# Turning the recurrence's queries and keys on VectorE and through DRAM instead of on TensorE

## The chip, the cores and the metric

One core of a Trainium2 chip runs the whole program: TensorE (PE; its weight loads are PEld), VectorE (DVE), ScalarE (ACT), GpSimd (POOL) and SyncE (SP), each with its own instruction stream, and DMA queues beside them. The metric is the device time of one execution in microseconds; lower is better. The kernel before takes 2662.75 us (median of 3 runs, 2661.4 to 2662.98).

## The reference, cut to what matters

Two transformer blocks over 256 tokens of width 2048, all float32. The first block projects the normalized input by `w_in` into nine parts; the change concerns the two that feed a gated linear recurrence with 8 heads of 128 channels:

```python
log_f = jnp.log(lb + (1.0 - lb) * jax.nn.sigmoid(z))     # z = h @ w_in, the hf columns
k  = (1.0 - lb) * jax.nn.sigmoid(-z)
qf = jax.nn.silu(q) * (HGRN_DK ** -0.5)                  # q = h @ w_in, the hq columns
...
o_inter = einsum('bhtk,bhkv->bhtv', q_c * exp(b_c), state)      # b_c: running sum of log_f in a chunk
scores  = einsum('bhtk,bhsk,bhtsk->bhts', q_c, k_c, decay)
```

Everything else (window attention, branch products, two feed-forward parts, a top-k mixer and a forgetting mixer) is unchanged.

## The kernel before

The 256 tokens are two tiles of 128. Each projection is cut into chunks of 512 output columns, and each chunk into pieces of 256 input rows. SP loads a piece into a staging half page (`stg`; four halves as a rule). ScalarE casts it to a rounded high part (L283, `ring`), VectorE subtracts to get the low part (L289, which also frees the staging half), and TensorE runs three products per 128 input rows and tile, always in the order A (high by high), B (high by low weight), C (low by high), 512 columns each (L335). A piece so serves 6 products of tile 0 and then 6 of tile 1. Product B cannot start before the piece's low part is there.

The order on every engine is fixed when the program is built. The planner walks the products in order; it emits the cast of a piece when its products are at most 12 units of modelled time away and the subtraction at 11 (`AHEAD_HI`, `AHEAD_LO`). Small work (evacuations, softmax, the recurrence) is written as generators that are pumped once per tick of 1.4 modelled us; `yield n` puts their next part n ticks later. What a generator emits lands between the casts, subtractions and products of that moment, and each engine then runs its list strictly in order.

The first block's order of chunks is hq (first four heads' queries), hf (their gates and keys), hi, hg, then keys and values of the attention, its queries and gates; later the second group of four heads: hq, hf, hi, hg. For a group:

- `head_hq`: after a tile's hq chunk, ScalarE applies Silu (L700) into `q`; four ticks later TensorE turns the four heads by four 128x128 transposes into one PSUM bank (`heads_T`, L350), and ScalarE copies the bank, scaled, into `G["qk"]` (L706).
- `head_hf`: waits for the bounds `lb` and `1-lb`, which POOL loads from `d_lb` (L724); then sigmoids (L730, L731), products with the bounds on VectorE (L734, L735) and POOL (L736), Ln and the rounded high part on ScalarE (L742, L743), the low part on VectorE (L744), and seven ticks later two banks of transposes for the keys, copied by ScalarE (L751).
- `hgrn`: two generators per group; POOL multiplies q by k (L804), TensorE forms running sums (L813, L814), ScalarE exponentiates (L817), POOL and VectorE multiply (L820, L821), TensorE forms the scores (L827).

`prep_lb` computes the bounds once; they are turned on TensorE, copied by VectorE (L494) and written to `d_lb` by POOL (L496). POOL then loads the table of running-sum patterns (L1691, `in_c_L`) and the masks (L1693, `in_c_pick`); ScalarE casts the first (L1695) and POOL the second (L1696). `prep_rope` (L452 to L470) puts a run of some twenty small instructions on VectorE at the same time.

The feed-forward parts already use another way to turn a 128x512 tile: VectorE transposes 32x32 blocks, POOL writes the tile to DRAM, and POOL reads it back with the blocks moved:

```python
nc.vector.transpose(ts, src)                                            # L366, flip_out
self.mq.dma_start(d, ts)                                                # L370
self.mq.dma_start(tr.rearrange("p (i x) -> p i x", i=4),
                  d.rearrange("(i r) (j x) -> (r j) i x", i=4, j=4))    # L376, flip_in
```

`FLIP_OUT` is 5 ticks and `FLIP_IN` 10. A read waits on POOL's queue until its write has landed.

## Time and profile before

| What | Value |
|---|---|
| Time, median of 3 runs | 2662.75 us |
| The profiled execution's own time | 2657.43 us |
| Its span | 2655.6 us |
| PE busy | 2623.4 us (99%) |
| DVE / ACT / POOL busy | 1613.8 (61%) / 1339.5 (50%) / 361.8 us (14%) |
| L335 products | 10824, 2508.7 us busy |
| L350 transposes | 252, 40.8 us busy |
| L366 / L370 / L376 (the existing turns) | 66 each |
| Mean granted TensorE clock | 0.998 |

TensorE is busy nearly all of the span, so a change matters by what it takes from TensorE's list and by what it makes TensorE wait for. Busy shares of the other engines say little: what counts is when a piece's cast and subtraction are done relative to the product that needs them. Times of rows below are microseconds from the start of the span.

### The profile page before, as it was taken

To read this page: it belongs to the slowest core of one execution; us is meant where nothing else is said; L and a number is where in the kernel's file an instruction comes from. 1 tells how busy PE (TensorE), PEld (TensorE's weight loads), DVE (VectorE), ACT (ScalarE), POOL (GpSimd) and SP (SyncE) were. 2 spreads that over 40 slices of the span, in tenths; PEclk is the share of its full clock that TensorE was granted. 3 is DMA by queue.
4 is the path that set the end of the run, shared out by engine and by line. 5 is a ranking of instruction groups with operands and counts; after the bars stand their busy time and mean duration, and the time that the engine had idled before them with its cause. 6 is when DMAs were issued, how large, how long until landed. Compare 5 with 4: busy or idle time off the path is not lost.

```text
span 2655.6 us, 32471 instructions
## 1 busy us (share of the span) xinstructions
PE 2623.4 (99%) x11929; PEld 2168.9 (82%) x11929; DVE 1613.8 (61%) x2145; ACT 1339.5 (50%) x2004; POOL 361.8 (14%) x420
## 2 busy tenths in 40 slices
PE   8999999999999999999999999999999999999998
PEld 7887788888888888888887788788888888888887
DVE  6765676465555454545457564855557757575757
ACT  6545654454553443443435574554556636464644
POOL 1341031020100000000001110100013212121211
PEclk9999999999999999999999999999999999999999
DMA  7545445666676565656566666456556766575754
GB/s 256 165 129 171 161 147 185 221 230 243 219 243 219 212 210 206 217 201 223 209 209 220 235 213 184 137 175 214 191 198 235 250 221 237 209 242 207 246 202 146
DMA packets 154431, 547.02 MB, mean 206 GB/s; under 512 B 19512, under 2 KB 22096, under 8 KB 153248
## 3 DMA queue, kind: packets, MB, share of 16 engines
q1 hardware_dynamic: 133504, 476.83, 51.9%
q0 software_dynamic: 19472, 67.54, 7.8%
q8 instruction: 93, 1.52, 0.2%
q10 hardware_dynamic: 1296, 0.59, 0.1%
q14 instruction: 66, 0.54, 0.1%
HBM read 514.46 MB, written 30.43 MB: 205 GB/s over the span
## 4 chain that ended last, share of the span: by engine, by line
PE 95%; ACT 1%; DVE 1%; POOL 1%; issue 1%; DMA 0%; SPq 0%; ACTq 0%; POOLq 0%; DVEq 0%
PE mm L335 89%; PE sd L350 1%; PE sd L827 1%; DVE ring L289 1%; ACT ring L283 0%; PE sd L1272 0%; PE sd L1349 0%; POOL s L820 0%; ACT s L394 0%; PE sd L670 0%; PE sd L1381 0%; PE sd L627 0%; PE sd L1244 0%; DMA s<-in_x_dram 0%; PE sd L813 0%
## 5 line engine op out<-in xcount | busy, mean ns | idle before, releaser
L335 PE MATMUL mm<-ring,s 128*128 128x512 f32 (+1 forms) x10824 | 2508.7, 391 | 8.0 <-ACT ring L283 6.3
L335 PEld LDWEIGHTS mm<-ring,s 128*128 128x128 f32 x10824 | 2023.4, 188 | 430.8 <-ACT ring L283 7.6
L289 DVE TENSOR_TENSOR ring<-stg,ring 128x1024 fp32r<-128x1024 f32 (+1 forms) x904 | 1088.9, 1252 | 406.2 <-ACT ring L283 399.4
L283 ACT CAST ring<-stg 128x1024 fp32r<-128x1024 f32 (+1 forms) x904 | 904.5, 1049 | 159.3 <-PE mm L335 93.8
L370 POOL DMA_DIRECT2D flip<-s x66 | 37.0, 562 | 973.0 <-DVE s L366 967.4
L1231 ACT ACTIVATE s<-mm,ss 128x512 f32<-128x512 f32 x60 | 41.5, 691 | 237.6 <-PE mm L335 224.9
L1068 DVE TENSOR_TENSOR s<-mm,s 128x512 f32<-128x512 f32 x72 | 48.7, 687 | 86.5 <-PE mm L335 86.3
L1020 ACT ACTIVATE s<-mm,ss 128x512 f32<-128x512 f32 x22 | 15.2, 690 | 139.1 <-PE mm L335 139.1
L1033 DVE SCALAR_TENSOR_TENSOR s<-mm,ss,s 128x512 f32<-128x512 f32 x22 | 16.1, 730 | 108.3 <-PE mm L335 108.3
L345 POOL TENSOR_TENSOR small<-small,mhalf 128x1 f32<-128x1 f32 (+1 forms) x27 | 17.5, 649 | 361.3 <-DVE small L344 328.7
L820 POOL TENSOR_TENSOR s<-s,s 128x512 f32<-128x512 f32 x32 | 53.3, 1672 | 93.8 <-ACT s L817 89.1
L356 ACT CAST s<-sd 64x256 fp32r<-64x256 f32 (+2 forms) x34 | 16.0, 470 | 88.6 <-PE sd L350 49.7
L376 POOL DMA_DIRECT2D s<-flip x66 | 50.5, 767 | 67.8 <-DMA flip<-s 39.8
L394 ACT ACTIVATE s<-sd,cols 128x128 fp32r<-128x128 f32 x160 | 45.8, 388 | 22.0 <-PE sd L350 19.1
L357 DVE TENSOR_TENSOR s<-s,s 128x512 fp32r<-128x512 f32 x22 | 15.2, 690 | 65.3 <-ACT s L356 65.3
L1584 POOL TENSOR_TENSOR s<-s,s 128x512 f32<-128x512 f32 x22 | 41.2, 1874 | 82.9 <-DVE s L1567 82.8
L350 PE MATMUL sd<-ident,s 128*128 128x128 f32 x252 | 40.8, 285 | 9.9 <-DMA ident<-in_c_ident_dram 4.0
L350 PEld LDWEIGHTS sd<-ident,s 128*128 128x128 f32 x252 | 32.4, 147 | 20.7 <-DMA ident<-in_c_ident_dram 4.0
L1565 ACT ACTIVATE s<-s,cols 128x256 f32<-128x256 f32 x88 | 48.2, 594 | 1.5
L357 DVE TENSOR_TENSOR s<-sd,s 64x256 fp32r<-64x256 f32 (+2 forms) x34 | 18.7, 549 | 47.4 <-ACT s L356 47.3
L1587 ACT CAST s<-s 128x512 fp32r<-128x512 f32 x22 | 13.6, 620 | 66.7 <-POOL s L1584 66.7
L366 DVE STREAM_TRANSPOSE s<-s 128x512 f32<-128x512 f32 x66 | 46.2, 706 | 1.6
(293 smaller groups left out, 1247.4 us busy)
## 6 DMA issues: line engine op xcount, KB each, us to landing
stg<-in_w_in_dram SPq DMA_DIRECT2D x232, 512.0 KB, 4.4
stg<-in_w_gu_dram SPq DMA_DIRECT2D x176, 512.0 KB, 5.5
stg<-in_w_dn_dram SPq DMA_DIRECT2D x176, 512.0 KB, 5.4
stg<-in_w_up_dram SPq DMA_DIRECT2D x176, 512.0 KB, 5.3
flip<-s POOLq DMA_DIRECT2D x66, 256.0 KB, 2.6
s<-flip POOLq DMA_DIRECT2D x66, 256.0 KB, 5.7
stg<-in_w_out_dram SPq DMA_DIRECT2D x32, 512.0 KB, 5.7
stg<-in_w_pg_dram SPq DMA_DIRECT2D x32, 512.0 KB, 5.5
```

The source lines that it names most:

```text
L283: nc.scalar.copy(w[:, 0, :, 0 : cc.n], stg[n_hi][0][:, :, 0 : cc.n])
L289: nc.vector.tensor_tensor(wl[:, :, 0 : cc.n], unstage(n_lo)[:, :, 0 : cc.n], wh[:, :, 0 : cc.n].bitcast(F32), op=ALU.subtract)
L335: nc.tensor.matmul(c.ps[t][:, 0 : c.n], xl if p == "C" else xh, wl if p == "B" else wh, start=n == 0, stop=n == 6 * c.nhp - 1)
L350: self.nc.tensor.transpose(bank[:, a * P : (a + 1) * P], s, self.ident)
L366: nc.vector.transpose(ts, src)
L376: self.mq.dma_start(tr.rearrange("p (i x) -> p i x", i=4), d.rearrange("(i r) (j x) -> (r j) i x", i=4, j=4))
L394: nc.scalar.activation(hi[:, a], b3[:, a], AF.Copy, scale=g[a])
L820: nc.gpsimd.tensor_tensor(k3, d3, kt[:, None, :].to_broadcast([P, 4, P]), op=ALU.mult)
L1068: nc.vector.tensor_tensor(y, ps[t], y, op=ALU.add)
L1231: nc.scalar.activation(r, ps[t], AF.Copy, scale=self.rs[t])
L1565: nc.scalar.activation(v, u, AF.Identity, scale=w[2], bias=self.cols[:, C_CB + k : C_CB + k + 1])
L1584: nc.gpsimd.tensor_tensor(o, o, g, op=ALU.mult)
```

## The change

The transposes of `head_hq` and `head_hf` leave TensorE: each of the eight 128x512 tiles (two of queries and two of keys in each of two groups) goes through `flip_out` and `flip_in`, and ScalarE copies from the tile that came back. Since 32x32 blocks come back in another order, the hq and hf columns of `w_in` are permuted on the host, `prep_lb` writes the bounds in that order by four DMAs instead of one, and the high and low parts of log f are written back in the old order through strided views. `hgrn` waits, when the program is built, until the copies have been emitted. The matrix products are unchanged in number.

```diff
 prep_lb
-        self.mq.dma_start(self.d_lb.rearrange("a (h k) -> (a h) k", h=8), q)
+        for n in range(4):
+            self.mq.dma_start(bass.AP(tensor=self.d_lb.tensor, offset=self.d_lb.offset + 512 * n, ap=[[32, 4], [P, 4], [1, 32]]),
+                              q[4 * n : 4 * n + 4].rearrange("p (j r) -> p j r", j=4))
...
 head_hq
-            yield 4
-            bank = yield from self.get("sd")
-            self.heads_T(q, bank)
-            self.drop(q)
-            nc.scalar.activation(G["qk"][:, 0:1024].rearrange("p (h n) -> p h n", h=4)[:, :, t * P : (t + 1) * P],
-                                 bank.rearrange("p (h n) -> p h n", h=4), AF.Copy, scale=P ** -0.5)
-            self.put("sd")
+            ts, d = yield from self.flip_out(q)
+            yield FLIP_OUT
+            tr = yield from self.flip_in(d)
+            self.drop(ts)
+            yield FLIP_IN
+            nc.scalar.activation(self.heads(G["qk"][:, 0:1024], t), tr.rearrange("p (i a q) -> p a i q", i=4, a=4), AF.Copy,
+                                 scale=P ** -0.5)
...
 head_hf
-                nc.scalar.copy(hi[:, u], fs[2 * u])
-                nc.vector.tensor_tensor(lo[:, u], fs[2 * u], hi[:, u].bitcast(F32), op=ALU.subtract)
-            yield 7
+                f4 = fs[2 * u].rearrange("p (j h r) -> p j h r", j=4, h=4)
+                hi4, lo4 = (z[:, u].rearrange("p (h r j) -> p j h r", h=4, j=4) for z in (hi, lo))
+                nc.scalar.copy(hi4, f4)
+                nc.vector.tensor_tensor(lo4, f4, hi4.bitcast(F32), op=ALU.subtract)
...
-                self.heads_T(fs[2 * u + 1], bank)
...
+                outs.append((yield from self.flip_out(fs[2 * u + 1])))
+            yield FLIP_OUT
...
+                trs.append((yield from self.flip_in(d)))
+            yield FLIP_IN
+            for u in range(2):
+                nc.scalar.copy(self.heads(G["qk"][:, 1024:2048], u), trs[u].rearrange("p (i a q) -> p a i q", i=4, a=4))
...
 hgrn
+        for f in (f"q{g}0", f"q{g}1", f"k{g}"):
+            yield from self.wait(f)
...
 _layout
+    for z in (1536, 2560):
+        w_in[:, z : z + 1024] = w_in[:, z : z + 1024].reshape(2048, 2, 4, 4, 32).swapaxes(2, 3).reshape(2048, 1024)
```

On TensorE the only difference is that eight banks of transposes are gone; on SP nothing moves. Three places on the other engines matter for the prediction.

VectorE, first group, around the gates. Before, from the second tile's products with the bounds (L734, L735) on; `ring_575` is the low part of the fourth piece of the chunk hi:

```order
L734 TENSOR_TENSOR s_55_586<-s_55_586,s_54_583 128x512
L735 SCALAR_TENSOR_TENSOR s_55_586<-s_55_586,s_54_583 128x512
L744 TENSOR_TENSOR s_56_599<-s_54_583,s_56_599 128x512
L744 TENSOR_TENSOR s_56_599<-s_55_586,s_56_599 128x512
L289 TENSOR_TENSOR ring_575<-stg_126,ring_575 128x1024
```

The same place of the changed kernel (L740, L741 are the products, L752 the low parts, `ring_577` is the same piece):

```order
L740 TENSOR_TENSOR s_56_588<-s_56_588,s_55_585 128x512
L741 SCALAR_TENSOR_TENSOR s_56_588<-s_56_588,s_55_585 128x512
L752 TENSOR_TENSOR s_57_601<-s_55_585,s_57_601 128x4x128
L752 TENSOR_TENSOR s_57_601<-s_56_588,s_57_601 128x4x128
L366 STREAM_TRANSPOSE s_56_588<-s_55_585 128x512
L366 STREAM_TRANSPOSE s_56_588<-s_56_588 128x512
L289 TENSOR_TENSOR ring_577<-stg_126,ring_577 128x1024
```

The two block transposes of the keys stand between the gates and the piece's subtraction.

POOL, first group, before: the bounds written (L496), the two tables loaded, the masks cast, the bounds read back (L724):

```order
L345 TENSOR_TENSOR small<-small,mhalf 128x1
L540 COPY ss_77<-small 128x1
L496 DMA d_lb<-s_31_311 16x128
L1691 DMA s_46_489<-in_c_L_dram 128x1152
L1693 DMA s_47_491<-in_c_pick_dram 128x1024
L1696 CAST pm<-s_47_491 128x1024
L724 DMA s_54_583<-d_lb 128x512 x2
```

And of the changed kernel, from the first tile's write on (L345 and L542 make the second tile's normalization factor):

```order
L370 DMA flip_392<-s_31_311 128x512
L345 TENSOR_TENSOR small<-small,mhalf 128x1
L542 COPY ss_77<-small 128x1
L370 DMA flip_411<-s_40_409 128x512
L497 DMA d_lb<-s_31_311 4x4x32 x4
L376 DMA s_31_311<-flip_392 128x4x128
L376 DMA s_40_409<-flip_411 128x4x128
L1706 DMA s_47_489<-in_c_L_dram 128x1152
L1708 DMA s_48_491<-in_c_pick_dram 128x1024
L1711 CAST pm<-s_48_491 128x1024
L730 DMA s_55_585<-d_lb 128x512 x2
```

The loads of both tables now stand behind five more DMAs, and a write of a flip stands ahead of the second tile's factor.

ScalarE, first group, before: the table cast, four pieces cast, then the gates' sigmoids:

```order
L1695 CAST s_45_488<-s_46_489 128x1152
L283 CAST ring_527<-stg_121 128x1024
L283 CAST ring_543<-stg_121 128x1024
L283 CAST ring_559<-stg_126 128x1024
L283 CAST ring_575<-stg_126 128x1024
L730 ACT_TABLE_LOAD
L730 ACTIVATE s_54_583<-mm_408,ss_77 128x512
```

And of the changed kernel, where L711 are the two copies of the queries:

```order
L1710 CAST s_46_488<-s_47_489 128x1152
L283 CAST ring_527<-stg_121 128x1024
L283 CAST ring_543<-stg_121 128x1024
L283 CAST ring_559<-stg_126 128x1024
L711 ACTIVATE s_37_389<-s_31_311 128x4x128
L711 ACTIVATE s_37_389<-s_40_409 128x4x128
L283 CAST ring_577<-stg_126 128x1024
L736 ACT_TABLE_LOAD
L736 ACTIVATE s_55_585<-mm_415,ss_77 128x512
```

The copies of the queries moved from right after their products to just ahead of the last cast before the sigmoids.

## Rows read from the trace of the kernel before

**Rows 1.** Waits of TensorE over the span: total, times, longest, all us
```profile
PE mm L335 <- ACT ring L283: 6.3, 3, 3.7
PE mm L335 <- DVE ring L289: 1.5, 2, 1.0
```

**Rows 2.** Chain in order of time, first group: start us, us, what
```profile
40.08 0.44 PE sd L350 x4
...
42.35 25.88 PE mm L335 x114
...
70.48 13.64 PE mm L335 x60
...
88.65 0.84 PE sd L827 x8
```

**Rows 3.** Costliest groups of the page, and its DMA issues with landing
```profile
L376 POOL DMA_DIRECT2D s<-flip x66 | 50.5, 767 | 67.8 <-DMA flip<-s 39.8
...
L366 DVE STREAM_TRANSPOSE s<-s 128x512 f32<-128x512 f32 x66 | 46.2, 706 | 1.6
...
flip<-s POOLq DMA_DIRECT2D x66, 256.0 KB, 2.6
s<-flip POOLq DMA_DIRECT2D x66, 256.0 KB, 5.7
```

**Rows 4.** DMA issues by line, the read of the bounds
```profile
s<-d_lb POOLq DMA_DIRECT2D x4, 256.0 KB, 4.2
```

**Rows 5.** Timeline of VectorE, first group: start, us, engine, line, operation, idle before
```profile
40.41 1.23 DVE L289 TENSOR_TENSOR ring<-stg,ring 128x1024 fp32r<-128x1024 f32 x1 [1.46 <-ACT ring L283]
...
63.23 0.69 DVE L734 TENSOR_TENSOR s<-s 128x512 f32<-128x512 f32 x1 [1.92 <-ACT s L730]
...
69.48 0.69 DVE L744 TENSOR_TENSOR s<-s,s 128x512 fp32r<-128x512 f32 x1 [0.75 <-ACT s L743]
70.08 5.17 DVE L289 TENSOR_TENSOR ring<-stg,ring 128x1024 fp32r<-128x1024 f32 x4
```

**Rows 6.** Timeline of ScalarE, first group
```profile
38.75 0.69 ACT L700 ACTIVATE s<-mm,ss 128x512 f32<-128x512 f32 x1
...
53.62 1.16 ACT L1695 CAST s<-s 128x1152 fp32r<-128x1152 f32 x1 [2.92 <-DMA s<-in_c_L_dram]
...
60.14 1.05 ACT L283 CAST ring<-stg 128x1024 fp32r<-128x1024 f32 x1 [0.21 <-DMA stg<-in_w_in_dram]
...
62.50 0.69 ACT L730 ACTIVATE s<-mm,ss 128x512 f32<-128x512 f32 x1
...
72.19 1.07 ACT L751 COPY s<-sd 128x512 f32<-128x512 f32 x2
...
81.43 0.69 ACT L767 ACTIVATE s<-mm,ss 128x512 f32<-128x512 f32 x1
```

**Rows 7.** Timeline of POOL, first group
```profile
39.03 0.56 POOL L345 TENSOR_TENSOR small<-small,mhalf 128x1 f32<-128x1 f32 x1 [5.22 <-DVE small L344]
...
48.09 0.57 POOL L1691 DMA_DIRECT2D s<-in_c_L_dram  x1
48.65 0.54 POOL L1693 DMA_DIRECT2D s<-in_c_pick_dram  x1
55.69 1.04 POOL L1696 CAST pm<-s 128x1024 uint8<-128x1024 f32 x1 [6.50 <-DMA s<-in_c_pick_dram]
...
85.64 1.80 POOL L820 TENSOR_TENSOR s<-s,s 128x512 f32<-128x512 f32 x1 [11.47 <-ACT s L817]
```

**Rows 8.** Timeline of VectorE, second group
```profile
323.05 4.62 DVE L289 TENSOR_TENSOR ring<-stg,ring 128x1024 fp32r<-128x1024 f32 x4
```

**Rows 9.** Timeline of TensorE, second group
```profile
322.99 3.00 PE L335 MATMUL mm<-ring,s 128*128 128x512 f32 x12
```

**Rows 10.** TensorE by stretches: us, busy (instructions), granted clock, DMA share, GB/s
```profile
1441.60:1445.50 3.90, 0.20 (x1) 1.00 0.71 255
1445.50:1448.40 2.90, 2.88 (x7) 0.50 0.41 90
```

More of the change, by code (lines that the diff above doesn't have):

```diff
@@ L686, in grp, with heads @@
         return self.hg[g]
-    def heads_T(self, src, bank):
-        self.transposes(bank, [src[:, a * P : (a + 1) * P] for a in range(4)])
+    @staticmethod
+    def heads(v, t):
+        return v.rearrange("p (h t i q) -> p h t i q", h=4, t=2, i=4)[:, :, t]
     def head_hq(self, c, g):
@@ L742, in done @@
                 nc.scalar.activation(fs[2 * u], fs[2 * u], AF.Ln)
[L743 to L745 removed]
+                f4 = fs[2 * u].rearrange("p (j h r) -> p j h r", j=4, h=4)
+                hi4, lo4 = (z[:, u].rearrange("p (h r j) -> p j h r", h=4, j=4) for z in (hi, lo))
+                nc.scalar.copy(hi4, f4)
+                nc.vector.tensor_tensor(lo4, f4, hi4.bitcast(F32), op=ALU.subtract)
             while "qk" not in G:
                 yield 1
+            outs = []
             for u in range(2):
[L749 to L755 removed]
+                outs.append((yield from self.flip_out(fs[2 * u + 1])))
+                self.drop(fs[2 * u])
+            yield FLIP_OUT
+            trs = []
+            for ts, d in outs:
+                trs.append((yield from self.flip_in(d)))
+                self.drop(ts)
+            yield FLIP_IN
+            for u in range(2):
+                nc.scalar.copy(self.heads(G["qk"][:, 1024:2048], u), trs[u].rearrange("p (i a q) -> p a i q", i=4, a=4))
+            self.drop(*trs)
+            self.flags.add(f"k{g}")
         return done
```

10 lines of the change are left out of this document (3 added, 7 removed).

## The prediction

> **What bounds the kernel now.** I read the page for the engines' shares first, then the waits of TensorE, then the chain in order of time through the first block, then the timelines of the four engines around the places that the change touches, because the share alone would mislead. TensorE is the bound, and over the whole span it waited only 6.3 us for casts and 1.5 us for low parts [rows 1]. So anything taken off TensorE's list is gained in full, and any wait made for it is lost in full. The reader should see in the chain that the first group's part is nothing but products, with banks of transposes between them [rows 2], and in the timelines that VectorE and ScalarE meet their deadlines there with very little to spare.
>
> **What is removed.** Eight banks of four transposes. The chain gives 0.44 us to a bank [rows 2], so 8 x 0.44 = 3.5 us leave TensorE; four banks are the first group's, four the second's, 1.76 us each. The eight copies from PSUM become eight copies from SBUF, which I price alike: 1.07 us for two [rows 6].
>
> Here the Trainium skill speaks against the change. The page VectorE: DVE Perf Modes, section Rules for kernel authors, says to turn 128x128 on TensorE if a PSUM destination will do, and in The three transpose paths it gives 390 ns to one on TensorE in isolation; by that price alone the 32 would free an estimated 12.5 us. In the chain four of them take 0.44 us, so the measured 3.5 us stands in the sum, and by the page's price the total below would come out near zero.
>
> **What is added beside other work.** Eight block transposes on VectorE at 0.71 us [rows 3], eight writes and eight reads on POOL's queue, landing after 2.6 and 5.7 us [rows 3], 4 MB in all. VectorE and POOL have idle time, so these cost nothing as work. The three more writes of the bounds cost an issue each, nearest 0.54 to 0.57 us [rows 7]. Strided writing of log f I price at nothing, since the block copies of the page's turns are strided too; a bound from above is one more pass of 0.69 us per low part [rows 5], which would go into the waits below. What matters is what stands behind the new instructions.
>
> **First group, step 1: the table comes later.** Before, the first tile's Silu ends at 38.75 + 0.69 = 39.44 [rows 6]. Now VectorE turns it to about 40.2. The second tile's factor (0.56 us and a small copy) started at 39.03 [rows 7]; it now stands behind that turn on VectorE and behind the flip's write on POOL and starts near 40.8, so the second Silu runs from 41.65 instead of 40.27, and its turn ends at about 43.05. Behind it on VectorE waits the subtraction that started at 40.41 [rows 5], then the small rope instructions, then the copy that the write of the bounds needs. All of these come 2.6 us later. On POOL the load of the table stood right behind that write, at 48.09 [rows 7]; it comes 2.6 us later, plus three writes (1.7), plus two reads of flips (2 x 0.77 [rows 3]) = 53.9. Its data took 53.62 - 48.09 = 5.5 us before [rows 6, 7]. The two reads, 0.5 MB, go down the same queue just ahead of it, and the masks' load took 7.0 us (48.65 to 55.69) behind the table [rows 7]; I take 6.6 us, between the two, so ScalarE's cast of the table starts at 60.5 instead of 53.62.
>
> Behind this cast on ScalarE stand the pieces of the chunk hi. The table's cast holds ScalarE about 1.06 us and a piece's about 0.98 (one is 1.05, overlapping the next). The second piece is then cast at 62.6 and subtracted by 63.85. Its products started at 42.35 + 90 x 25.88 / 114 = 62.8 [rows 2]; two banks less bring that to 61.9. TensorE waits about 2.0 us, for the cast and then for the low part, where it waited for nothing.
>
> **Step 2: the fourth piece comes later still.** ScalarE casts the third piece (64.5), copies the two query tiles (65.6), casts the fourth (66.5), loads a table (1.28) and starts the sigmoids at 67.8; before it was 62.50 [rows 6], so 5.3 us later. The masks land at about 54.5 + 8 = 62.5; with their cast (1.04) and two issues the bounds arrive about 64.6 + 4.2 = 68.8 [rows 4, 7], which costs a tenth more. From the sigmoids the gates took until 69.48 + 0.69 = 70.17 [rows 5], now 75.6. Behind them stand two block transposes, 1.4 us, and only then the fourth piece's subtraction: from 76.9 to 78.1. Its product B was due at 70.48 + 7 x 0.227 = 72.1 [rows 2], with a margin of 0.7 us over the subtraction that ended about 71.4 (a quarter of the 5.17 us after 70.08) [rows 5]. With four banks gone it is due at 70.3. So TensorE waits 78.1 - 70.3 = 7.8 us by then, the 2.0 us of step 1 among them, the rest in one wait of almost 6 us.
>
> If the table comes no later than before, only the two copies (1.1) and two transposes (1.4) push the subtraction: it ends at 73.8 and the wait is 3.5 us. If the table takes as long as the loads and reads at their slowest, 2 to 3 us more, the wait is 10 to 11 us. I keep 3.5 and 11 as ends and take 7.8.
>
> **Step 3: the clock.** After a stretch of 3.9 us in which TensorE did only 0.20 us of work, the granted clock was 0.50, the lower of its two levels, for 2.9 us [rows 10]. At half speed that loses 1.45 us, and a little more until full speed is back; I take 1.7 us once, after the wait of step 2. From below it is nothing, if no stretch is idle long enough; from above twice that.
>
> **Step 4: the keys.** Their turns end at about 77, the writes land by 80, the reads by 86. ScalarE reaches the two key copies only after the hi evacuation, which started at 81.43 [rows 6] and is bound to TensorE: 81.43 - 1.76 + 9.5 = 89.2. So the landing is hidden by 3 us. But the copies, 1.07 us, now stand ahead of the first exponential. POOL's product came 85.64 + 1.80 - 81.43 = 6.0 us after that evacuation [rows 6, 7], and TensorE's use at 88.65 [rows 2] left about a microsecond; I price what is left at 0.2 us.
>
> **Second group.** The same order with no table in the way: one query copy (0.55) and two block transposes (1.4) stand ahead of the first subtraction of the four that started at 323.05 [rows 8]. It then ends near 326.2. Its piece starts with the second six of the twelve products at 322.99 [rows 9], product B at 324.6; without the two banks of keys that is 323.7. TensorE waits 2.5 us. Ends: 1 us, if the softmax beside it leaves slack, and 4 us. The query flips are long back by then.
>
> **Sum.** -3.5 + 7.8 + 1.7 + 0.2 + 2.5 = +8.7 us. The profiled execution took 2657.43 us of its own, 1.8 more than the span and 5.3 less than the median, so 2666.1 for it, and 2671.5 against the median of 2662.75. With the ends of the terms: -3.5 + 3.5 + 0 + 0 + 1 = +1 and -3.5 + 11 + 3.4 + 0.5 + 4 = +15.4; not all go one way, so this case's own range is 2665.5 to 2677.
>
> **The rivals.** First: the table's load is not late. POOL's queue was idle between its DMAs and the loads of weights pause while VectorE is held, so the data may come in the shadow. Then steps 1 and 2 make 3.5 us: -3.5 + 3.5 + 1.7 + 2.5 = +4.2, 2667.0. Against it: the load needs the copy behind the rope, and that is behind both turns.
>
> Second, on the other side: TensorE's relief is all that counts. The place is the fourth piece's subtraction; it decides whether this ends before 70.3. Against the first rival it would have to be 3.5 us earlier still, by the pieces' weights arriving sooner (their casts before the sigmoids waited for DMA, 0.21 us before the last [rows 6]) and by two PSUM copies less ahead of them. Then nothing is lost, the second group's deadline is met too, and the time is 2662.75 - 3.5 = 2659.2. For it speaks that TensorE waited so little in the whole program [rows 1]; against it, that the margin was 0.7 us.
>
> Third: the flips' reads come late behind the weights and ScalarE stands at the key copies. From a landing of 89.2 on, each microsecond is one on TensorE; 3 us of it and a late table make +14, 2676.8.
>
> **How the numbers follow.** About 0.2% (5.3 us) is what a measurement of this kernel can tell from no change. Forecast 0.55, first rival 0.22, second 0.13, third 0.10. The forecast lies past +5.3 us in all but a tenth of its cases, the first rival in a third: slower 0.68. The second rival reaches -5.3 us only if a bank was worth more than 0.44 and the small waits of the recurrence go too: faster 0.05; the same 0.27. The range for 8 in 10 is 2662.5 to 2677.5: it takes in the first rival and leaves most of the second and the worst of the third out.
>
> **What would show it.** In the changed kernel's waits of TensorE: two to three waits near 62 us for cast and low part, one of 4 to 7 us near 72 for L289 in VectorE, then a lower granted clock for some 3 us; one of 1 to 4 us near 324. On ScalarE the table's cast near 60.5 behind its DMA, on VectorE the two transposes right ahead of the late subtraction. No transposes of L350 between 38 and 71. If TensorE waits under 2 us by 75, steps 1 and 2 are wrong and the time is below 2663; if the table is cast by 56, step 1 is.

## The result, and the profile after

The changed kernel takes 2676.05 us (median of 4 runs, 2674.24 to 2677.69), the kernel before, run on the same chip, 2662.07 (4 runs, 2660.82 to 2662.98): 14.0 us slower, ratio 1.0051, 95% interval 1.0039 to 1.0063. The forecast was 2671.5 in a range of 2662.5 to 2677.5. The sign, the places and the order of events came out; the size did not, 14.0 us for 8.7.

One sentence of the section on the change is wrong: the strided views write the parts of log f in the order in which the turned channels come to lie on the partitions, not in the old one. No step of the working rests on it. And a name: TensorE runs 12 products to a piece and 96 to a chunk, and the product that waited for `ring_577` was its 242nd, so the piece that the text ahead calls the fourth of the chunk hi is its fifth. The recorded expectations use the same names, so "fourth" and "fifth" stand below for that piece and the next; the times are those of the piece meant.

TensorE's waits over the whole span, to be read beside [rows 1]; the columns are total, times, longest:

```profile
PE mm L335 <- ACT ring L283: 9.9, 4, 3.7
PE mm L335 <- DVE ring L289: 8.9, 5, 3.5
PE sd L350 <- ACT ring L283: 2.4, 1, 2.4
```

Casts went from 6.3 to 9.9 us, low parts from 1.5 to 8.9: 11.0 more. Where they stand, in the timeline of TensorE (start, us, instructions, the wait before them):

```profile
65.39 0.50 PE L335 MATMUL mm<-ring,s 128*128 128x512 f32 x1 [3.63 <-ACT ring L283]
66.64 11.34 PE L335 MATMUL mm<-ring,s 128*128 128x512 f32 x36 [0.76 <-DVE ring L289]
81.47 13.94 PE L335 MATMUL mm<-ring,s 128*128 128x512 f32 x53 [3.49 <-DVE ring L289]
...
337.75 1.46 PE L335 MATMUL mm<-ring,s 128*128 128x512 f32 x5 [3.20 <-DVE ring L289]
```

Three places: 3.63 + 0.76 us for chunk hi's second piece, 3.49 us for its fourth, 3.20 us in the second group. Before, TensorE waited at none of the three. The other engines at the first two places, ScalarE first, then VectorE, then POOL (to be read beside [rows 5 to 7]):

```profile
63.23 1.15 ACT L1710 CAST s<-s 128x1152 fp32r<-128x1152 f32 x1 [10.52 <-DMA s<-in_c_L_dram]
67.13 1.15 ACT L711 ACTIVATE s<-s 128x512 f32<-128x512 f32 x2
70.53 0.69 ACT L736 ACTIVATE s<-mm,ss 128x512 f32<-128x512 f32 x1
```

```profile
77.98 1.12 DVE L752 TENSOR_TENSOR s<-s,s 128x512 fp32r<-128x512 f32 x1 [0.78 <-ACT s L751]
79.00 1.30 DVE L366 STREAM_TRANSPOSE s<-s 128x512 f32<-128x512 f32 x2
80.23 4.60 DVE L289 TENSOR_TENSOR ring<-stg,ring 128x1024 fp32r<-128x1024 f32 x4
```

```profile
53.79 0.57 POOL L1706 DMA_DIRECT2D s<-in_c_L_dram  x1
64.30 1.04 POOL L1711 CAST pm<-s 128x1024 uint8<-128x1024 f32 x1 [9.40 <-DMA s<-in_c_pick_dram]
```

The table's load is issued at 53.79 (48.09 before), its cast starts at 63.23 (53.62 before) behind a landing of 9.4 us; the sigmoids follow at 70.53 (62.50 before), and the fourth piece's subtraction stands at 80.23 right behind the two block transposes.

TensorE by stretches, with the columns of [rows 10] (us, TensorE's busy time, ..., granted clock, DMA share, GB/s):

```profile
66.00:72.80 6.80, 6.16 (x15) 4.82 (x16) 4.50 (x7) 6.77 (x10) 1.28 (x2) 0.50 0.82 261
83.10:86.40 3.30, 3.30 (x10) 2.53 (x9) 1.83 (x3) 1.04 (x1) 1.33 (x2) 0.50 0.91 323
339.10:342.40 3.30, 3.30 (x7) 1.94 (x7) 2.02 (x3) 1.48 (x4) 1.39 (x2) 0.50 0.93 304
452.00:455.30 3.30, 3.30 (x10) 2.57 (x9) 3.30 (x5) 0.73 (x1) 0.10 (x1) 0.54 0.20 68
```

Behind each of the three places the granted clock was 0.50, the lower level, for 3.3 us, behind the first for twice that. Half of the busy time is lost: 6.16 / 2 = 3.1 us, and twice 1.65. The last row follows a wait that the change didn't make (2.4 us at 448, 2.1 us before); before, the clock stayed at 1.00 there.

So the profiled spans (2655.6 and 2672.5, +16.9) add up: banks -3.5, waits 7.9 + 3.2, half clock 3.1 + 1.65 + 1.65, the fourth stretch 1.65 + 0.3; together +16.0, and 0.9 is spread. The page shows the two sides: L350 with 32 transposes less (252 and 40.8 us before), and L335, whose number is the same and whose 2508.7 us grew by half clock:

```profile
L335 PE MATMUL mm<-ring,s 128*128 128x512 f32 (+1 forms) x10824 | 2515.2, 392 | 18.9 <-ACT ring L283 9.9
L350 PE MATMUL sd<-ident,s 128*128 128x128 f32 x220 | 35.9, 286 | 10.2 <-DMA ident<-in_c_ident_dram 4.2
```

The profiled execution of before was among its fastest (2657.43; single executions in all the comparisons below took 2656.9 to 2667.3), which is why its profile lies 16.9 us from the other one and the medians 14.0. One execution of experiment 12 ran at a granted clock of 0.60 on average and took 4113.56 us; it counts in the median of the table below and not in the ratio.

### The profile page after: what moved, and what is told of

Its sections match the earlier page's. It is cut to its first block, busy times and chain, and to the rows that moved or that the text cites. A ratio compares the mean times of both kernels' runs of the same rounds, so it can differ in the third digit from the quotient of the medians.

```text
span 2672.5 us, 32451 instructions
## 1 busy us (share of the span) xinstructions
PE 2629.1 (98%) x11897; PEld 2169.8 (81%) x11897; DVE 1619.9 (61%) x2153; ACT 1340.9 (50%) x2004; POOL 372.4 (14%) x439
## 4 chain that ended last, share of the span: by engine, by line
PE 91%; ACT 2%; DVE 2%; issue 2%; POOL 1%; DMA 1%; SPq 0%; ACTq 0%; POOLq 0%; DVEq 0%
PE mm L335 86%; ACT ring L283 1%; PE sd L350 1%; PE sd L842 1%; DVE ring L289 1%; POOL s L835 0%; PE sd L1287 0%; PE sd L1364 0%; DMA s<-in_c_L_dram 0%; ACT s L394 0%; PE sd L672 0%; PE sd L1396 0%; PE sd L629 0%; PE sd L1259 0%; DMA s<-in_x_dram 0%
## 5 line engine op out<-in xcount | busy, mean ns | idle before, releaser
L335 PE MATMUL mm<-ring,s 128*128 128x512 f32 (+1 forms) x10824 | 2515.2, 392 | 18.9 <-ACT ring L283 9.9
L335 PEld LDWEIGHTS mm<-ring,s 128*128 128x128 f32 x10824 | 2028.1, 189 | 446.3 <-ACT ring L283 11.6
L370 POOL DMA_DIRECT2D flip<-s x74 | 41.6, 563 | 1020.5 <-DVE s L366 1011.9
L345 POOL TENSOR_TENSOR small<-small,mhalf 128x1 f32<-128x1 f32 (+1 forms) x27 | 17.5, 649 | 356.3 <-DVE small L344 324.2
L376 POOL DMA_DIRECT2D s<-flip x74 | 56.6, 766 | 65.1 <-DMA flip<-s 32.8
L366 DVE STREAM_TRANSPOSE s<-s 128x512 f32<-128x512 f32 x74 | 51.7, 706 | 8.9 <-ACT s L704 7.2
L350 PE MATMUL sd<-ident,s 128*128 128x128 f32 x220 | 35.9, 286 | 10.2 <-DMA ident<-in_c_ident_dram 4.2
L400 DVE SCALAR_TENSOR_TENSOR s<-sd,cols,s 128x128 fp32r<-128x128 f32 x160 | 44.0, 342 | 3.0 <-ACT s L394 3.0
```

Source lines behind the costliest of these rows:

```text
L335: nc.tensor.matmul(c.ps[t][:, 0 : c.n], xl if p == "C" else xh, wl if p == "B" else wh, start=n == 0, stop=n == 6 * c.nhp - 1)
L350: self.nc.tensor.transpose(bank[:, a * P : (a + 1) * P], s, self.ident)
L376: self.mq.dma_start(tr.rearrange("p (i x) -> p i x", i=4), d.rearrange("(i r) (j x) -> (r j) i x", i=4, j=4))
L400: nc.vector.scalar_tensor_tensor(lo[:, a], b3[:, a], g[a], hi[:, a].bitcast(F32), op0=ALU.mult, op1=ALU.subtract)
```

## The experiments

Each was timed against the kernel before on the same chip; its ratio (of the means) and interval are to that. An interval reaches 2 to 4.5 us to either side, so theories that lie closer together are told apart by the traces and not by the time.

| Kernel | Time, us | Before, us | Ratio, interval |
|---|---|---|---|
| changed | 2676.05 | 2662.07 | 1.0051, 1.0039 to 1.0063 |
| 1 tables first | 2673.42 | 2661.31 | 1.0049, 1.0037 to 1.0062 |
| 2 subtraction first | 2678.82 | 2661.31 | 1.0068, 1.0055 to 1.0080 |
| 3 banks left out of before | 2662.63 | 2661.31 | 1.0008, 0.9999 to 1.0016 |
| 4 order mended | 2684.76 | 2661.31 | 1.0100, 1.0084 to 1.0117 |
| 5 reads after tables | 2675.46 | 2660.63 | 1.0055, 1.0042 to 1.0068 |
| 6 queries only | 2671.22 | 2660.63 | 1.0036, 1.0022 to 1.0050 |
| 7 second group only | 2667.43 | 2660.63 | 1.0019, 1.0010 to 1.0028 |
| 8 order mended again | 2678.94 | 2660.63 | 1.0065, 1.0052 to 1.0077 |
| 9 tables in the middle | 2672.16 | 2661.97 | 1.0038, 1.0026 to 1.0051 |
| 10 and gates later | 2668.59 | 2661.97 | 1.0028, 1.0018 to 1.0037 |
| 11 banks left out, gates later | 2661.54 | 2661.97 | 1.0000, 0.9992 to 1.0009 |
| 12 as 10, copies later | 2671.46 | 2661.61 | 1.0033, 1.0020 to 1.0046 |

**1. Tables first.**

```diff
-                yield 4
+                yield 16
                 nc.scalar.copy(self.L[:, 0 : 9 * P], raw[:, 0 : 9 * P])
...
+                self.spawn(L())
                 self.spawn(self.prep_lb())
...
-                yield 6
-                self.spawn(L())
             self.spawn(later())
```

> The changed kernel, with POOL's two loads of the recurrence's tables issued at the start of its list instead of behind the writes of the bounds and the reads of the turned queries; nothing else moves on any engine. Theory 'order' (work comes late because of what stands ahead of it): ScalarE casts the table before 56 us instead of at 63.2, and the first two waits of TensorE near 62 to 67 us (3.6 and 0.8) go with the 6.7 us at half clock that follow. The fourth piece's subtraction still stands behind the copies of the queries and the two block transposes, and ends at 75 to 75.6 against a use that comes at 70.4: one wait of 4.5 to 5.2 us near 71, then about 3.3 us at half clock (1.65 lost). The second group keeps its 3.2 us and its 1.65. Sum -3.5 + 4.9 + 1.65 + 4.85 = +7.9, so about 2670 (2668.5 to 2671.5). Theory 'traffic' (the turns' bytes crowd the memory, so that weights and tables come late wherever they stand): a wait of about 3 us for a cast stays near 62 and the time is within 2 us of 2676.

Measured: 2673.42, above the 2671.5 that "order" allowed and inside no theory's band. TensorE's timeline:

```profile
11.98 1.97 PE L350 MATMUL sd<-ident,s 128*128 128x128 f32 x8 [5.29 <-DMA s<-in_x_dram]
...
80.16 14.84 PE L335 MATMUL mm<-ring,s 128*128 128x512 f32 x53 [6.68 <-DVE ring L289]
```

The first two waits are gone; the table is cast at 55.95. But POOL had nothing ahead of the loads, so they ran at the start beside the input's, and the first products came 3.0 us later (5.29 us of waiting for `in_x` where 2.39 stood). And the fourth piece's wait grew from 3.49 to 6.68: with TensorE no longer held up at the second piece, it reached the fourth sooner than the subtraction did. Removing one wait handed most of it to the next.

**2. Subtraction first.**

```diff
+            yield 2
             outs = []
...
-            yield FLIP_OUT
+            yield FLIP_OUT - 2
```

> The changed kernel, with the keys' two block transposes two ticks later on VectorE and everything behind them at its old place: in both groups one subtraction of a weight piece passes ahead of the two transposes, and nothing else moves on any engine. Theory 'order': the first waits (3.6 and 0.8) and their half clock stay; the wait near 78 shrinks by the 1.3 us of the transposes from 3.5 to 2.2, the one near 335 from 3.2 to 1.9, and the half clock behind each may stay or go: 2673.4 if both stay, 2670.1 if both go. Theory 'bystanders' (the late subtraction waits for its cast or its data, and the transposes fill time that it would have waited anyway): 2676 and the same waits.

Measured: 2678.82, by the medians 17.5 us over before (14.0 for the changed kernel; the intervals overlap), so no gain, which neither theory gave. TensorE's timeline:

```profile
81.87 12.35 PE L335 MATMUL mm<-ring,s 128*128 128x512 f32 x53 [2.67 <-DVE ring L289]
101.12 1.97 PE L843 MATMUL sd<-s,s 128*128 128x64 f32 x8 [2.37 <-POOL s L836]
...
340.62 1.43 PE L335 MATMUL mm<-ring,s 128*128 128x512 f32 x5 [1.78 <-DVE ring L289]
346.04 2.08 PE L672 MATMUL sd<-s,s 128*128 128x512 f32 x2 [3.99 <-ACT s L665]
```

The two waits for subtractions did shrink, to 2.67 and 1.78, so the transposes are no bystanders. But two new ones, 2.37 for POOL's product of keys (L836) and 3.99 for ScalarE's L665, took more than that. ScalarE, ahead of the first of them:

```profile
89.36 1.05 ACT L283 CAST ring<-stg 128x1024 fp32r<-128x1024 f32 x1 [2.97 <-DMA stg<-in_w_in_dram]
...
94.64 1.13 ACT L767 COPY s<-s 128x512 f32<-128x512 f32 x2
```

The copies of the keys (L767) waited for nothing, so this is not the third rival. ScalarE's casts ahead of them waited for weights, and the copies came 1.25 us later than in the changed kernel (93.39); TensorE, this time without half clock behind the subtraction, stood at the scores' running sums 1.2 us sooner (94.06 for 95.25). In the second group the writes of the turned keys came later by the edit, and L665's tile was still being written to DRAM: L666 right behind it waited 0.70 us for such a write, and 4 shows the same wait of L665.

**3. Banks left out of before.**

```diff
-            bank = yield from self.get("sd")
-            self.heads_T(q, bank)
+            bank = q
...
-                bank = yield from self.get("sd")
-                self.heads_T(fs[2 * u + 1], bank)
+                bank = fs[2 * u + 1]
```

> The kernel before, with the eight banks of four transposes on TensorE left out and nothing in their place: ScalarE's copies read the queries and keys as they lie, so the recurrence gets them unturned. All other engines' lists are unchanged. This is what the removal alone is worth. By the chain's 0.44 us to a bank it is 3.5 us, 2658.6; by the group's mean of 0.162 us for each of 32 transposes 5.2 us, 2656.9. By the margin theory (the fourth piece of the chunk hi was 0.7 us early, and TensorE comes there 1.8 us sooner) a wait of about 1.1 us appears near 70 and perhaps another in the second group, so 2659 to 2661.

Measured: 2662.63, no gain at all (0.9999 to 1.0016).

```profile
73.79 13.98 PE L335 MATMUL mm<-ring,s 128*128 128x512 f32 x53 [3.19 <-DVE ring L289]
```

At the fourth piece TensorE now waited 3.19 us for VectorE and lost about 1.7 more at half clock. The margin theory had the place and was short on the size (1.1 us). What made the size is not the deadline alone. Product B was due at 70.6, 1.5 us sooner than before (72.1), against a margin of 0.7; but the subtraction also ended 2.4 us later than before, though nothing had been put ahead of it. VectorE's list ran 1.1 us later in this execution (L494 at 47.95 for 46.85), and the bounds landed late, by 1.3 more:

```profile
65.74 0.69 DVE L732 TENSOR_TENSOR s<-s 128x512 f32<-128x512 f32 x1 [3.21 <-DMA s<-d_lb]
```

So that the removal alone brings nothing here is shown by the time; that the earlier deadline is the reason, only in part. The 3.5 us that the change was to free could not be had from this order even for nothing.

**4. Order mended.** The edit of 1, and

```diff
             yield from self.wait("lb")
+            yield 2
...
-            yield FLIP_IN
+            yield FLIP_IN + 5
             nc.scalar.activation(self.heads(G["qk"][:, 0:1024], t), ...
...
+            yield 2
             outs = []
...
-            yield FLIP_OUT
+            yield FLIP_OUT - 4
```

> The changed kernel with four things moved and nothing added: tables loaded first on POOL, the gates' sigmoids and products two ticks later (so that one more weight piece is cast and subtracted ahead of them), the keys' block transposes two ticks later still (behind one more subtraction), the copies of the queries five ticks later (behind the gates on ScalarE). Theory 'order': the three waits near 62, 78 and 335 us and the half clock behind them go, and at most 0 to 2 us are left near 73; -3.5 + 0 to 2, so 2658.6 to 2660.6, faster than the changed kernel by 15 to 17 us and at or just below the kernel before. Theory 'traffic': the same bytes move at the same places, so waits for casts stay and the time is above 2668.

Measured: 2684.76, the slowest of all; "order" failed as I had applied it.

```profile
98.83 1.97 PE L844 MATMUL sd<-s,s 128*128 128x64 f32 x8 [5.25 <-POOL s L837]
...
345.07 2.08 PE L672 MATMUL sd<-s,s 128*128 128x512 f32 x2 [7.08 <-ACT s L665]
```

ScalarE's list at the two places:

```profile
91.38 0.62 ACT L768 COPY s<-s 128x512 f32<-128x512 f32 x1 [1.07 <-DMA s<-flip]
...
344.43 0.59 ACT L665 COPY s<-sd 128x512 f32<-128x512 f32 x1 [4.12 <-DMA flip<-s]
```

Of the three waits of the changed kernel 0.9 + 1.4 + 0.9 us were left by 80 us and nothing in the second group's subtraction, as forecast. In their place stood 5.25 us for the scores, with ScalarE standing at the key copies for the reads to land (1.07 us, and 0.86 at the second: the third rival's mechanism), and 7.08 us for L665: ScalarE held its whole list for a tile that a turn's write (L370) was still reading, and that write had been moved back by my own two ticks.

**5. Reads after tables.**

```diff
-            yield FLIP_OUT
+            yield FLIP_OUT + 3
             tr = yield from self.flip_in(d)
...
-            yield FLIP_IN
+            yield FLIP_IN - 3
```

> The changed kernel, with POOL's two reads of the turned queries issued behind its loads of the two tables instead of ahead of them; no other engine's list moves. Theory 'order': without 0.5 MB ahead of it in the queue the table needs about 5.5 us again; issued near 52.2 it is cast at 57.7 to 58.5 instead of 63.2, and TensorE's waits near 62 to 67 us with their 6.7 us at half clock go. What is left is what the kernel with early tables showed, a wait of 5 to 6.7 us for the fourth piece's low part, its half clock, and the second group's 3.2 + 1.65, but without that kernel's 2.9 us at the start: 2669.5 to 2671.5. Theory 'traffic' (what counts is how many bytes POOL's queue and the weights ask for in these 10 us, not their order): the table still takes 8 to 9 us, a wait of 1 to 3 us for the cast stays and the time is 2673 to 2676.

Measured: 2675.46, as the changed kernel, in the band of "traffic" but not by its mechanism: the wait for a cast was gone. The table was cast at 60.34, 7.0 us after its issue (between the theories' 5.5 and 8 to 9), the first wait fell to 0.64, and the fourth piece's rose to 9.78. TensorE, and VectorE's first product with the bounds:

```profile
81.99 14.62 PE L335 MATMUL mm<-ring,s 128*128 128x512 f32 x53 [9.78 <-DVE ring L289]
```

```profile
71.93 0.69 DVE L740 TENSOR_TENSOR s<-s 128x512 f32<-128x512 f32 x1 [4.98 <-DMA s<-d_lb]
```

This shows a second late chain beside the table's: the masks land late too, POOL casts them, and only behind that cast does it issue the bounds' read; VectorE stood 4.98 us for the bounds. In the changed kernel ScalarE's lateness covered this.

**6. Queries only.** `head_hf` and `prep_lb` are those of before, and

```diff
-    for z in (1536, 2560):
+    for z in (1536,):
```

The turned queries' channels then lie in another order than the keys', so this kernel's scores are not the reference's.

> Only the queries are turned on VectorE and through DRAM; the keys keep their four banks on TensorE, the bounds their one write and the gates their plain layout. Theory 'order': the table comes 1.7 us sooner than in the changed kernel (three writes less ahead of it), cast near 61.5, so a first wait of about 2.7 us; the fourth piece's subtraction has no block transposes and no strided writes ahead of it, so the second wait is about 2.7 us; 1.65 us of half clock behind one or both; the second group's wait is under 1 us. -1.76 + 5.4 + 1.65 to 3.3 + 0.5 = +5.8 to +7.4, so 2668 to 2669.5. Theory 'keys' (the keys' turn makes the loss, the queries' is free because nobody waits for them before 85 us): -1.76, 2660.3.

Measured: 2671.22 (2665.55 to 2675.7, a wide spread), above the 2668 to 2669.5 of "order", far above the 2660.3 of "keys". So the queries' turn alone, which nobody needs before 85 us, costs 10.6 of the 14.0 us by the medians (5.9 to 13.3 by the interval), by what it pushes back. TensorE waited 1.07 + 0.76 at the second piece, then 3.20 at a bank of keys (L350), for POOL's product with bounds that had come late.

**7. Second group only.** The first group has the lines of before, and the second group's bounds are written once more, turned, after the first group has read its own:

```diff
+            if g == 0:
+                bank = yield from self.get("sd")
+                self.heads_T(q, bank)
...
-    for z in (1536, 2560):
+    for z in (2048, 3072):
```

> Only the second group of four heads is turned on VectorE and through DRAM; the first group keeps its banks, its tables' place, its plain bounds and its plain gates. Theory 'order': no wait near 62 or 72; near 335 the changed kernel's wait of 3.2 us and its 3.3 us at half clock (1.65 lost). -1.76 + 3.2 + 1.65 = +3.1, 2664.4. Theory 'first group alone' (all of the loss comes from the table and its followers, and the second group's wait was a late effect of it): -1.76, 2659.6.

Measured: 2667.43 (1.0010 to 1.0028); "first group alone" falls.

```profile
326.50 1.43 PE L335 MATMUL mm<-ring,s 128*128 128x512 f32 x5 [3.20 <-DVE ring L289]
```

```profile
328.00:331.50 3.50, 3.50 (x7) 2.14 (x8) 1.85 (x2) 0.37 (x1) 1.25 (x2) 0.53 0.90 267
440.00:446.00 6.00, 6.00 (x23) 4.83 (x22) 5.08 (x9) 1.38 (x2) 0.77 (x1) 0.72 0.50 162
```

The wait is 3.20 us, to the hundredth that of the changed kernel, with its half clock. The profiled span is 4.8 us over that of before: the +3.1 forecast and another 1.6 from the half clock at 440 to 446 (a clock of 0.72 on average), the stretch behind the wait that was there before. The medians differ by 6.8, the means by 5.1. The other 2 us go with half clock: the three executions with a granted clock of 0.997 or 0.998 on average took 2662.2 to 2663.1, the eight with 0.994 to 0.996 took 2665.1 to 2668.4, and the profile is of one of the three.

**8. Order mended again.** Against the changed kernel:

```diff
-            yield FLIP_OUT
+            yield FLIP_OUT + 3
             tr = yield from self.flip_in(d)
...
-            yield FLIP_IN
+            yield FLIP_IN + 7
             nc.scalar.activation(self.heads(G["qk"][:, 0:1024], t), ...
...
             yield from self.wait("lb")
+            yield 2
...
+            yield 2
             outs = []
...
-                self.drop(ts)
-            yield FLIP_IN
+            yield FLIP_IN + 3
+            self.drop(*[o[0] for o in outs])
             for u in range(2):
...
-        yield 2 + 4 * w
         for f in (f"q{g}0", f"q{g}1", f"k{g}"):
             yield from self.wait(f)
+        yield 4 * w
```

> All eight turns stay. Moved against the changed kernel: the reads of the queries behind the tables' loads, the gates two ticks later (one more weight piece cast and subtracted ahead of them), the keys' block transposes two more ticks later (behind one more subtraction), the copies of the queries behind the gates, the keys' reads given three more ticks before they are copied, the recurrence started only after that copy, and the keys' turned tiles held until their write has landed for certain. Theory 'order': the second mended order failed only where ScalarE stood at the keys' copies and at a tile still being written, and with both given time nothing is left but 1 to 3 us of short waits near 73 to 79: -3.5 + 1 to 3, 2659.5 to 2661.5, equal to the kernel before. Theory 'starved' (while VectorE is held by gates and turns no staging half comes free, the weights come late and TensorE pays for each microsecond of it somewhere in the next 30 us, whatever the order): 2667 to 2673.

Measured: 2678.94; "starved" had the band (2667 to 2673) too low as well. VectorE again waited 4.12 us for the bounds, TensorE 4.98 for a cast at 78.6, and the recurrence, started later, waited 2.08, 2.32 and 2.89 at 124, 161 and 197 us. Too many things had moved for one verdict; the next kernels moved one or two at a time.

**9. Tables in the middle.**

```diff
-                yield 4
+                yield 9
                 nc.scalar.copy(self.L[:, 0 : 9 * P], raw[:, 0 : 9 * P])
...
                 self.spawn(self.prep_rope())
-                yield 6
+                yield 1
                 self.spawn(L())
```

> The changed kernel, with POOL's two loads of the tables issued behind the second write of a turned query (near 44 us, where the weights' loads pause) and ahead of the writes of the bounds; no other engine's list moves. Theory 'order, two chains' (ScalarE's casts wait for the first table and the bounds' read waits behind the cast of the masks; both must come early): as with the loads at the start of the list, but without that kernel's 2.9 us at the start: waits near 62 to 67 gone, one wait of 5 to 6.7 us for the fourth piece near 71 with 1.65 to 3 us of half clock, the second group as before: 2669.5 to 2671. Theory 'traffic': the queries' reads (0.5 MB at 50 to 56 us) still hold the weights back, so that the casts wait for data and nothing is gained: 2673 to 2676.

Measured: 2672.16, between the theories' bands (to 2671, from 2673); the interval holds both. Both chains are mended (table cast at 52.92, bounds' read issued at 55.09), the start is free, and the fourth piece waited 6.54 us. ScalarE's third and fourth casts of chunk hi:

```profile
60.81 1.05 ACT L283 CAST ring<-stg 128x1024 fp32r<-128x1024 f32 x1 [1.56 <-DMA stg<-in_w_in_dram]
63.73 1.05 ACT L283 CAST ring<-stg 128x1024 fp32r<-128x1024 f32 x1 [0.82 <-DMA stg<-in_w_in_dram]
```

They wait for weights (1.56 and 0.82 us), where before the last started at 60.14. So a third chain is left: weights that come late.

**10. And gates later.** As 9, with

```diff
             yield from self.wait("lb")
+            yield 2
             lb, om = yield from self.get("s2", 2)
...
-            yield FLIP_OUT
+            yield FLIP_OUT - 2
```

> As the kernel with the tables in the middle, and the gates two ticks later in both groups, so that the fourth piece is subtracted ahead of them on VectorE; the turns keep their place. Theory 'order': the fourth piece's wait goes, the fifth piece, now first behind gates and turns, is due 2.7 us later and still waits 3 to 4 us; the second group's wait falls from 3.2 to 0.5 and loses its half clock; with TensorE earlier the scores wait 2 to 4 us for keys that come no sooner. -3.5 + 3.5 + 1.65 + 0.5 + 3 = +5, 2665.7 (2664 to 2668). Theory 'one deadline' (the fourth piece was the only place without slack): -3.5 and at most 1, 2657.5 to 2659.

Measured: 2668.59, within what "order" allowed (to 2668) but for 0.6; "one deadline" falls.

```profile
74.42 0.51 PE L335 MATMUL mm<-ring,s 128*128 128x512 f32 x1 [1.68 <-ACT ring L283]
77.02 12.32 PE L335 MATMUL mm<-ring,s 128*128 128x512 f32 x41 [2.10 <-DVE ring L289]
...
333.77 2.07 PE L672 MATMUL sd<-s,s 128*128 128x512 f32 x2 [4.05 <-ACT s L665]
```

The fourth piece's 6.54 us became 1.68 + 2.10 at the fifth, 3.8 as forecast, and the scores waited for nothing; in the second group L665 took the place of the subtraction with 4.05 us.

**11. Banks left out, gates later.** As 3, with

```diff
             yield from self.wait("lb")
+            yield 2
...
-            yield 7
+            yield 5
```

> The kernel before with the eight banks left out (queries and keys unturned, as in the third experiment) and the gates two ticks later, so that the fourth piece is subtracted ahead of them; nothing else moves. Theory 'order': the 3.2 us that appeared at the fourth piece when the banks were left out, and the half clock behind it, go, and the removal at last shows its 3.5 us: 2657 to 2659. Theory 'given back' (the gates' chain on VectorE stops the freeing of staging halves, so the relief is lost to the next piece or to the scores): a wait of 1 to 3 us elsewhere between 70 and 95, 2660 to 2663.

Measured: 2661.54 (0.9992 to 1.0009): the band of "given back". The 3.19 us at the fourth piece are gone, as "order" said; at 267.8 us TensorE is 1.15 us ahead of before. In the second group it then waits 1.42 us for L663 (L665 of the changed kernel), and the old wait near 436 is followed by half clock in this execution. The old wait near 1446 is followed by 6.7 us of it, where before had 3.3, and another 3.3 us stand from 1472; together about 5 us are lost, more than the relief. By the interval at most 2.1 of the 3.5 us reach the time; how much of that stays open.

**12. As 10, copies later.** As 10, with

```diff
-            yield FLIP_IN
+            yield FLIP_IN + 9
             nc.scalar.activation(self.heads(G["qk"][:, 0:1024], t), ...
...
-                self.drop(ts)
             yield FLIP_IN
+            self.drop(*[o[0] for o in outs])
```

> As the kernel with tables in the middle and gates later, with two things more: ScalarE's copies of the turned queries nine ticks later (behind the gates instead of ahead of the sigmoids, in both groups), and the keys' turned tiles kept until the read has landed, so that the attention's copy L665 of the second group gets another tile and doesn't wait for a turn's write. All other lists keep their order; all eight turns stay. Theory 'order': in the second group ScalarE is free of 1.2 us of copies and 1.8 us of waiting ahead of L665, TensorE's wait of 4.05 us there falls below 1 and its 2.9 us of half clock go; in the first group the waits of 1.7 and 2.1 us near 73 fall by about 1 in all and the half clock behind them may go. 2668.6 - 6 to 9, so 2659.5 to 2662.5, equal to the kernel before with all turns in place. Theory 'starved' (VectorE's longer stretch without subtractions holds the weights' loads back, and TensorE pays for it wherever the copies stand): the first group keeps its 3.8 us and 3.3 us of half clock, and the second group waits 2 us or more at the next cast: 2665 to 2668.

Measured: 2671.46 (1.0020 to 1.0046); against 10 (1.0018 to 1.0037) no gain. "Order" fails in the first group; what "starved" named is there, with a band that was too low (2665 to 2668). ScalarE's fourth cast, and TensorE in the first group:

```profile
64.47 1.05 ACT L283 CAST ring<-stg 128x1024 fp32r<-128x1024 f32 x1 [2.05 <-DMA stg<-in_w_in_dram]
```

```profile
75.15 0.50 PE L335 MATMUL mm<-ring,s 128*128 128x512 f32 x1 [1.75 <-ACT ring L283]
77.97 11.96 PE L335 MATMUL mm<-ring,s 128*128 128x512 f32 x41 [2.32 <-DVE ring L289]
```

With 1.15 us of copies taken from ahead of it the cast came no sooner: it waited 2.05 us for its weights. The second group did as forecast at L665 (1.80 us for 4.05, and no half clock behind it), but then waited for the scores, with 6.7 us at half clock behind it (0.50 from 363.0 to 369.7):

```profile
362.36 1.46 PE L843 MATMUL sd<-s 128*128 128x64 f32 x8 [1.59 <-POOL s L836]
```

That takes back what L665 had given. The first group's 1.75 + 2.32 are the weights'. Why these come late is in the chain of staging: a load starts when a subtraction frees a half. VectorE's list from the end of the rope's small instructions, before:

```profile
46.85 0.27 DVE L494 COPY s<-sd 16x128 f32<-16x128 f32 x1
47.05 1.20 DVE L289 TENSOR_TENSOR ring<-stg,ring 128x1024 fp32r<-128x1024 f32 x1
```

and in kernel 10:

```profile
42.41 0.71 DVE L366 STREAM_TRANSPOSE s<-s 128x512 f32<-128x512 f32 x1 [2.42 <-ACT s L704]
49.45 0.27 DVE L494 COPY s<-sd 16x128 f32<-16x128 f32 x1
49.65 7.54 DVE L289 TENSOR_TENSOR ring<-stg,ring 128x1024 fp32r<-128x1024 f32 x5
```

The first block transpose pushes the second Silu back, the second transpose waits 2.42 us for it, and the rope and the subtractions behind come 2.6 us later; so does every load that they release, and these now meet the queries' reads (landing in 7.1 us there). No run took the transposes from ahead of the rope, so this last link is read from the traces and not shown by an experiment.

## Why the prediction was right in its path and short in its size

**The removal.** -3.5 us by the chain; nothing in the traces speaks against it as work taken off TensorE's list. As a gain it does not exist in this order: experiment 3 took it for nothing and got nothing (0.9999 to 1.0016). The second rival (relief is all that counts) is out by that run. The Trainium skill's rule (VectorE: DVE Perf Modes, Rules for kernel authors) to turn on TensorE where PSUM will do gave the right decision here, though not for its price: the 390 ns that the prediction took from the page are for bf16, and here four in fp32 took 0.44 us; leaving out all 32 moved the time by less than its interval.

**Step 1, the table.** The issue came at 53.79 for 53.9; the landing took 9.4 us for 6.6, the cast started at 63.23 for 60.5, and the wait was 4.4 us for 2.0. I had bounded the landing by the masks' 7.0 us, which had one load ahead of it; here two reads stood ahead. Experiment 5 took these away and the table landed in 7.0.

**Step 2, the fourth piece.** A total of 7.9 us for 7.8 by then. This is right by two errors: the subtraction ended at 81.4 for 78.1, and TensorE was 3.1 us later by half clock, which the working had put behind this wait instead of ahead of it. That the two block transposes hold the subtraction is shown by experiment 2 (3.49 to 2.67). Of the 3.3 us by which it ended late, 2.7 are the table's. The others are a term put at nothing: the strided writing of log f. L751 and L752 took 1.1 us each, where L743 and L744 had taken 0.62 and 0.69, and from the first sigmoid to the last low part the gates took 8.6 us for 7.7; in experiment 6, with plain gates, the two lines took 0.62 and 0.69 again. That the table alone makes the rest is false: experiments 1 and 9 removed it and the fourth piece still waited 6.5 to 6.7. The bounds and the weights were as late as the table, and the forecast named only the first of these two, at a tenth of a microsecond.

**Step 3, the clock: the step that failed.** "I take 1.7 us once." It is 6.4 us, paid at three places, at the first for 6.8 us on end. This term alone is 4.7 us of the 5.3 between forecast and medians, and of the 8.2 between forecast and profiled spans; the rest of those is the stretch near 450 (1.95), the second group (0.7) and the 0.9 that is spread. The bound from above ("twice that") was too low because I looked for one long wait; the wait of 3.2 us cost the same 1.65 as the one of 3.5.

**Step 4, the keys.** 0.2 us priced, nothing seen in the changed kernel, because TensorE was late there. With TensorE earlier the scores waited 5.25 us in experiment 4, ScalarE standing 1.07 and 0.86 us for the landing, and 2.37 in experiment 2 without that: the cover was the loss itself.

**Second group.** 2.5 us priced, 3.2 measured, and its half clock; experiment 7 shows it by itself. The 0.7 us more are about what the strided writing adds to the gates here (8.6 us for 7.7), by the trace; no run takes it out alone.

**The rivals.** The first (the table not late) is false by the trace. The third (flips late at the key copies) did not happen in the changed kernel, and was part of the price of the repair in 4. The best order found with all turns in place (experiment 10) is 6.6 us slower than before by the medians; none beat it.

## What to carry to other kernels

Where one engine is 99% busy and the others meet its deadlines by tenths of a microsecond, taking work off it moves its deadlines forward too: look first for the next thing that must then be early. A change that puts work on idle engines is priced by what stands behind that work in each list (another engine's table, a read of bounds, the freeing of a staging buffer), and several such chains can be late by the same amount, so that mending one shows the next. And every wait of a few microseconds on TensorE is to be priced with the half clock that can follow it, each one by itself.

## What the runs showed of the hardware

Half clock lasted 3.3 us behind waits of 3.2 to 3.5 us, and 6.8 us behind the 4.4 us of the changed kernel. In experiment 5 the clock fell 5.1 us before the wait of 9.8 us ended, and 5.1 us of work behind it ran at 0.50. A wait of 3 us is not needed: behind 2.4 us near 448 the changed kernel's clock fell, behind 2.1 us at the same place the profiled execution of before kept 1.00, and there experiment 11 lost it behind 2.3 and experiment 7 behind 2.0. Nor is one of 3 us sure to bring it. Behind the wait of 3.7 us near 1446, which the change doesn't touch, the clock was low for 3.3 us in before and stayed at 1.00 in experiment 3; in experiment 11 it was low for 6.7 us (experiment 3, then 11):

```profile
1446.00:1453.00 7.00, 3.73 (x21) 3.11 (x21) 5.23 (x15) 4.77 (x13) 2.22 (x5) 1.00 0.43 160
```

```profile
1445.00:1451.70 6.70, 5.72 (x16) 4.55 (x17) 4.12 (x12) 3.31 (x9) 2.06 (x5) 0.50 0.36 128
```

The Trainium skill (TensorE: Matmul & The Clock Gate, Part 1) says that the same kernel can meet the gate in different phases from run to run; these rows agree. It is a part of why single executions of the kernel before spread over 10 us: of the 20 beside experiments 9 to 11, the six with a granted clock of 0.997 or 0.998 on average took 2658.2 to 2659.8, the fourteen with 0.996 took 2661.2 to 2666.3.

The table's load of 576 KB on POOL's queue took 5.5 us before [rows 6, 7], 6.1 us in the pause of the weights (experiment 9), 7.0 with the masks behind it and the reads after it (experiment 5), 8.7 and 9.4 behind two reads of 256 KB (experiment 6 and the changed kernel). The changed kernel's DMA issues have this row (KB each, us to landing):

```profile
s<-in_c_L_dram POOLq DMA_DIRECT2D x1, 576.0 KB, 9.4
```
